# Matmul with batch norm: the last half chunk of the last column tile as one piece of 256 rows instead of two of 128

## The chip, the cores and the metric

The kernel runs on one core of a Trainium2 chip. The metric is the device time of one execution in microseconds; five runs of the kernel before have a median of 211.6 us (211.12 to 212.11).

## The reference

```python
batch, m, k, n = 16, 512, 1024, 768
y = np.matmul(x, weight)                       # x: (16, 512, 1024), weight: (1024, 768), float32
mean = np.mean(y, axis=(0, 1), keepdims=True)
var = np.var(y, axis=(0, 1), keepdims=True)
y_norm = (y - mean) / np.sqrt(var + eps)
return (gamma * y_norm + beta).astype(np.float32)
```

Mean and variance of each of the 768 columns go over all 8192 rows, so no column can be normalised before its last row has been multiplied. The output is 25.2 MB.

## The kernel before, in words

The 8192 rows are cut into 16 chunks of 512 (`C`, `CH`); half a chunk has 256 rows (`QR`). The 768 columns are six tiles of 128 (`NT`). The first two tiles are computed with rows on the partitions; the other four are column tiles: `y` lies transposed, with the tile's 128 columns on the partitions and the rows along the free dimension, so that statistics are taken along a partition. Each column tile goes through all chunks. For each chunk TensorE adds up eight matmuls into a PSUM bank, VectorE takes statistics of the bank (`bn_stats`), ScalarE copies it as bf16 into a `y` buffer (`keep`). When a tile's 16 chunks are done, the statistics are merged (`bn_aggr`), ScalarE takes the root, VectorE forms scale and shift. Then blocks of the tile are normalised in place, turned back to rows (transpositions on TensorE or by DMA), copied as float32 by ScalarE and stored through SP's queue. All of that but the last tile's goes on while TensorE multiplies the next tile.

The last tile (`nt = NT - 1`) has nothing to hide behind, so its end is made small:

- Its chunks 0 to 14 are as above. The last chunk, 15, is cut into `PIECES`, each with its own PSUM bank, matmuls, statistics and copy (`last_unit`, L694 on; the matmuls have line 705, the statistics 712, the copy 715). Before, the pieces are 256, 128 and 128 rows.
- The statistics of chunks 0 to 13 are merged early into the first three columns of `fin` (`sum_up`, L1145 to L1147). Chunk 14's go into the next six (L662), each piece's into six more. One `bn_aggr` over all of `fin` (`aggregate`, L1150) gives the tile's mean and variance. The `root` (L1153, ScalarE) follows, and on VectorE `first_term` (L1156) and `affine` (L1160 to L1162: reciprocal, scale, shift).
- Then blocks of this tile (`ends`): two of 256 rows, two of 512, six of 1024 and one of 512, each normalised (L1185, VectorE), turned (L1008, TensorE), copied (L1198, ScalarE) and stored (L1201, SP).
- One block of the tile before, of 1024 rows (`HELD = 1`), is held back until here. Its norm is done long before; its eight transpositions (L1008) stand on TensorE behind the last piece, its copy is line 1082 (ScalarE), its store line 1074 (SP, 512 KB).

No order of work is written by hand. Each step is a task with a due time, the engines it may use with an assumed occupation, and what it depends on. `arrange` runs an assumed timetable: in each round it takes the engine that can begin first, and among the tasks that can begin on it within 0.2 us (`LOOK`) the one with the smallest due time. It assumes 0.06 us from the end of a task to the start of one that depends on it (`SEM`). The instructions are then issued in this order, and each engine keeps it. The tasks around the change are:

```python
t = pe_task(0.92 * rows / QR, emit, waits(range(JW), c, 0, QPC), takes=[slot], uses=[x_slot[c]])
b = task(clock[0] - 40, dve(0.05 + 0.3 * rows / QR), bn, [t], uses=[slot])
k = task(clock[0] + 0.5, act(0.05 + 0.22 * rows / QR), keep, [b, col_end[nt, c - 1][1]], uses=[slot, y_of(nt, c)])
...
ag = task(E - 50.0, dve(0.25), aggregate,
ro = task(E - 50.0, {"ACT": (0.2, 0.3)}, root, [ag])
...
    b = col_block(hn, hc, E + 0.3 + 0.3 * i, hf)
    b.deps.append(col_end[nt, C - 1, len(PIECES) - 1][0])
```

`clock[0]` is the sum of TensorE's assumed occupations so far, `E` its value at the end of the last piece. A VectorE task ends 0.09 us after its occupation, one of TensorE 0.03. The last line makes the planner count the held block's transpositions (0.0555 us each) from the last piece's statistics on; the instructions themselves do not wait for these.

Of the kernel before, what the change touches and what calls it, by code (L numbers as in the profile page):

```python
# [227 lines left out]
def kernel(  # L228
# [10 lines left out]
    f32 = mybir.dt.float32  # L239
# [8 lines left out]
    P = 128  # L248
# [5 lines left out]
    QR = 256  # L254
    QPC = CH // QR
    JW = KQ // 64
    WAKE = 30
    FILL = 8
    EARLY = 4
# [1 line left out]
    GA = 2  # L261
    NA = GA * P
    GY = 2
    PAD = 34
    HELD = 1
    ASTAT = {2:tuple(range(4,16))}
    RC = C - 2
# [11 lines left out]
    singles = ctx.enter_context(tc.tile_pool(name="singles", bufs=1))  # L279
# [25 lines left out]
    ring = singles.tile([P, RING], f32)  # L305
    w_sb = singles.tile([P, JW, 2, N], bf16)
    eps_sb = singles.tile([P, 1], f32)
# [11 lines left out]
        seq(nc.vector.memset(acc, 0.0))  # L319
    tot = singles.tile([P, 2, NA], f32)  # L320
    stats = singles.tile([P, (NT - GA) * C + PAD, 6], f32)
    fin = singles.tile([P, 27], f32)
    psums = {nt: singles.tile([P, 2, C], f32, name=f"psums{nt}") for nt in ASTAT}
    sums = {nt: singles.tile([P, 4 + 6 * C], f32, name=f"sums{nt}") for nt in ASTAT}
    for nt in ASTAT:
# [18 lines left out]
    def task(prio, engines, emit, deps=(), lock=False, **kw):  # L344
        t = Task(prio, engines, emit, deps, **kw)
        t.lock = lock
        tasks.append(t)
        return t

    def dve(occ):  # L350
        return {"DVE": (occ, occ + 0.09)}
# [7 lines left out]
    def pe(occ):  # L359
        return {"PE": (occ, occ + 0.03)}  # L360
# [10 lines left out]
    def load_w(jw, jw1):  # L371
        def emit(eng):
            rows = weight.rearrange("(i jw c e) n -> i c jw (e n)", i=4, jw=JW, e=2)
            dst = w_sb.rearrange("p jw e n -> p jw (e n)")
            for i in range(4):
                seq(nc.gpsimd.dma_start(dst[32 * i:32 * i + 32, jw:jw1], rows[i, :, jw:jw1]))
# [18 lines left out]
    def turn_x(xslot, slot, m0, t0, jw0, jw1, new, rows=QR):  # L395
        def emit(eng):
            if new:
                xT_sb = xtpool.tile([P, JW, CH, 2], bf16, tag="xT")
                slot.tile = xT_sb
            half, row = divmod((m0 + 32 * t0) % CH, QR)  # L400
            src = xslot.tile[:, t0:t0 + rows // 32].rearrange("p t k -> p (t k)").bitcast(f32)
            src = src.rearrange("p (t jw c) -> p t jw c", jw=JW, c=32)
            dst = slot.tile.rearrange("p jw m e -> p (jw m e)").bitcast(f32)
            dst = dst.rearrange("p (jw q t r) -> p q t jw r", jw=JW, q=QPC, r=32)
            dst = dst[:, half, row // 32:(row + rows) // 32, jw0:jw1]
# [10 lines left out]
    for kind, n, *n1 in order:  # L416
        if kind == "w":
# [3 lines left out]
            t += 2.1 * (n1[0] - n)  # L421
            if n1[0] == JW:
                task(t, {"POOL": (0.6, 0.6)}, lambda eng: make_identity(nc, ident))
# [117 lines left out]
    def wake(count, slot):  # L541
        def emit(eng):
            idle_ps = psum.tile([P, CH], f32, tag="b")
            for _ in range(count):
                seq(nc.tensor.matmul(idle_ps, idle_sb[:, 0:P], idle_sb, start=True, stop=True))  # L545
        return emit
# [31 lines left out]
    def col_unit(nt, c, jws, q0=0, q1=QPC):  # L578
        slot = bank_of.setdefault((nt, c), None) or Slot(banks)
        bank_of[nt, c] = slot  # L580
        first = jws[0] == 0 and q0 == 0
        xs = [plain[c][0][jw] for jw in jws] if c in plain else [x_slot[c]]
        kw = {"takes": [slot], "uses": xs} if first else {"uses": [slot] + xs}
        t = pe_task((1.728 if c in plain else 1.808) * len(jws) / JW * (q1 - q0) / QPC,
                    mm(nt, c, list(jws), slot, q0, q1),
                    waits(jws, c, q0, q1) + ([plain[c][1][jw] for jw in jws] if c in plain else []), (nt, c), **kw)
        if q1 - q0 == QPC:
            t.hosts = 4
        if jws[-1] == JW - 1 and q1 == QPC:
            col_stats(nt, c, slot, t)  # L590
        return t
# [98 lines left out]
            k.deps.append(col_end[nt, c - 1][1])  # L690
        col_end[nt, c] = b, k

    PIECES = (0, QR), (QR, P), (QR + P, P)

    def last_unit(q):
        nt, c = NT - 1, C - 1
        r0, rows = PIECES[q]
        slot = Slot(banks)

        def emit(eng):  # L700
            y_ps = psum.tile([P, CH], f32, tag="b")
            slot.tile = y_ps
            for jw in range(JW):
                for e in range(2):
                    seq(nc.tensor.matmul(  # L705
                        y_ps[:, 0:rows], w_sb[:, jw, e, nt * P:(nt + 1) * P],
                        x_slot[c].tile[:, jw, r0:r0 + rows, e],
                        start=(jw == 0 and e == 0), stop=(jw == JW - 1 and e == 1),
                    ))

        def bn(eng):
            seq(nc.vector.bn_stats(fin[:, 9 + 6 * q:15 + 6 * q], slot.tile[:, 0:rows]))

        def keep(eng):
            seq(nc.scalar.copy(y(nt, c)[:, r0:r0 + rows], slot.tile[:, 0:rows]))
# [4 lines that stand above are left out]
        col_end[nt, c, q] = b, k  # L720


    wake_slot = Slot(banks)
    task(1.0, pe(0.217 * WAKE), wake(WAKE, wake_slot), takes=[wake_slot])

# [410 lines left out]
    for c in range(EARLY, C - 1):  # L1136
        for jws in halves:
            col_unit(nt, c, jws)
    for q in range(len(PIECES)):
        last_unit(q)  # L1140
# [18 lines left out]
    def affine(eng):  # L1159
# [6 lines left out]
    ag = task(E - 50.0, dve(0.25), aggregate,  # L1166
              [su, col_end[nt, C - 2][0]] + [col_end[nt, C - 1, q][0] for q in range(len(PIECES))])
    ro = task(E - 50.0, {"ACT": (0.2, 0.3)}, root, [ag])
    ft = task(E - 50.0, dve(0.1), first_term, [ag])
    af = task(E - 50.0, dve(0.45), affine, [ro, ft])  # L1170
    for i, (hn, hc, hf) in enumerate(held):
        b = col_block(hn, hc, E + 0.3 + 0.3 * i, hf)
        b.deps.append(col_end[nt, C - 1, len(PIECES) - 1][0])
    ends = [(0, 0, QR), (0, QR, QR), (1, 0, CH), (2, 0, CH)] + [(c, 0, 2 * CH) for c in range(3, C - 1, 2)]
    ends += [(C - 1, 0, CH)]
    for c, r0, rows in ends:
        due = E + 2.0 + 0.6 * c
        n = max(rows // CH, 1)
        keeps = [col_end[nt, c + i][1] for i in range(n) if c + i < C - 1]
        keeps += [col_end[nt, C - 1, q][1] for q in range(len(PIECES))] if c + n == C else []  # L1180
        norms = []
# [67 lines left out]
```

## Time and profile before

| | |
|---|---|
| median of five runs | 211.6 us (211.12 to 212.11) |
| the profiled execution: its own time | 212.11 us |
| its span, first to last instruction | 209.8 us |
| mean granted TensorE clock | 0.981 |
| busy: TensorE, VectorE, ScalarE, GpSimd | 192.9, 140.2, 153.8, 107.5 us |
| matmuls of the last chunk (L705): first start | 188.20 us |
| root of the last tile (L1153): start | 190.88 us |
| last copy of ScalarE: end | 200.2 us |
| transfers: last packets | 208.2 us |

A row of the profile names the line of the kernel, the engine, the operation, what is written from what, the shape, and how many instructions were merged (x24). PE is TensorE's matmul, PEld its weight load, DVE is VectorE, ACT ScalarE, POOL GpSimd; SPq is SP's queue, which issues the stores. In a timeline row the first number is the start and the second the length, in microseconds from the span's start; what ended an idle stretch stands in brackets. In a row of a group the numbers behind the bar are the busy time in us and the mean length of one instruction in ns. A window's row gives the busy time of each engine in it, then the clock, the share of the 16 DMA engines and GB/s. A matmul's record is longer than its share of TensorE, since matmuls overlap; how fast they follow each other is read from their starts.

The transfers of the program's own code are queues of the kind "instruction" in the profile: q8 has ten packets, 0.16 MB, and q14 seven, 0.06 MB.

### The profile page before, as it was taken

The numbers are of one execution on the slowest core, as the hardware profiler recorded it, in microseconds if no ns is written. First come the engines' busy times: TensorE is split into PE (matmuls) and PEld (weight loads), VectorE is DVE, ScalarE is ACT, GpSimd is POOL, SyncE is SP. The second block draws the span as 40 slices with busy tenths as digits, with TensorE's granted clock in tenths as the row PEclk, the third lists the DMA queues.
The fourth block names the chain that finished last, engine by engine and source line by source line (L and its number), as shares of the span: only waits on it lengthen the run. The fifth ranks groups of instructions, "written<-read, shape, count | busy, mean of one in ns | idle before, by whom it ended". The sixth has DMA issues, their size and how long they took to land.

```text
span 209.8 us, 3519 instructions
## 1 busy us (share of the span) xinstructions
PE 192.9 (92%) x1242; PEld 114.8 (55%) x1242; DVE 140.2 (67%) x230; ACT 153.8 (73%) x264; POOL 107.5 (51%) x130
## 2 busy tenths in 40 slices
PE   7988999999999999999999999999999999997600
PEld 2355554856568888776864444444444455545400
DVE  4220887787879899768879999854963594348500
ACT  2000665999999999989778987999676768878910
POOL 7777957697858999999106986750000000000000
PEclk9999999999999999999999999999999999999975
DMA  5999999999999999999004799999999999999994
GB/s 56 165 164 196 195 196 196 196 197 196 191 195 195 196 197 196 196 197 189 14 0 158 262 386 351 297 343 317 266 274 236 325 325 336 254 348 308 344 345 144
DMA packets 95137, 47.95 MB, mean 229 GB/s; under 512 B 20880, under 2 KB 94608, under 8 KB 95120
## 3 DMA queue, kind: packets, MB, share of 16 engines
q0 software_dynamic: 34688, 18.36, 64.1%
q1 hardware_dynamic: 60432, 29.37, 50.8%
q8 instruction: 10, 0.16, 0.3%
q14 instruction: 7, 0.06, 0.1%
HBM read 36.71 MB, written 25.17 MB: 295 GB/s over the span
## 4 chain that ended last, share of the span: by engine, by line
PE 78%; DMA 10%; ACT 3%; DVE 1%; issue 1%; POOL 1%; ACTq 0%; DVEq 0%; POOLq 0%
PE y_ps L529 50%; PE y_ps L467 21%; DMA ring<-in_x_dram 8%; PE y_ps L767 4%; ACT o_sb L1198 3%; DMA w_sb<-in_weight_dram 3%; PE o_ps L1008 2%; POOL ring L385 1%; PE y_ps L705 1%; DVE xT_sb L406 1%; PE a_ps L872 0%; ACTq L1244 0%; PE o_ps L1038 0%; PE tot_ps L825 0%; DVE y_sb L1185 0%
## 5 line engine op out<-in xcount | busy, mean ns | idle before, releaser
L529 PEld LDWEIGHTS <-w_sb 128*128 128x128 bf16 x512 | 49.4, 97 | 59.1
L529 PE MATMUL y_ps<-xT_sb,w_sb 128*128 128x512 bf16 (+1 forms) x256 | 59.5, 380 | 0.0
L529 PE MATMUL y_ps<-x_pl,w_sb 128*128 128x512 bf16 x256 | 58.7, 379 | 0.0
L385 POOL DMA_DIRECT2D ring<-in_x_dram x76 | 47.4, 628 | 12.7 <-DMA ring<-in_x_dram 4.6
L467 PE MATMUL y_ps<-w_sb,xT_sb 128*128 128x256 bf16 x448 | 50.7, 273 | 2.0 <-DVE xT_sb L406 1.3
L406 DVE STREAM_TRANSPOSE xT_sb<-ring 128x1024 f32<-128x1024 f32 (+1 forms) x35 | 38.3, 1131 | 17.2 <-DMA ring<-in_x_dram 17.2
L467 PEld LDWEIGHTS <-xT_sb 128*128 128x128 bf16 x448 | 43.5, 98 | 9.9 <-DVE xT_sb L406 2.0
L662 DVE BATCH_NORM_STATS2 stats<-y_ps 128x6 f32<-128x512 f32 x46 | 31.5, 691 | 23.0 <-PE y_ps L529 22.8
L666 ACT CAST y_sb<-y_ps 128x512 bf16<-128x512 f32 x51 | 29.0, 592 | 11.7 <-DVE stats L662 10.0
L501 ACT COPY x_pl<-xT_sb 128x1024 bf16<-128x1024 bf16 x32 | 32.4, 1050 | 2.3 <-DVE xT_sb L406 2.3
L610 ACT ACTIVATE sq_sb<-y_ps 128x512 f32<-128x512 f32 x28 | 16.6, 603 | 22.0 <-PE y_ps L467 21.4
L906 POOL TENSOR_TENSOR ring<-ring,sum 128x1024 f32<-128x1024 f32 (+1 forms) x11 | 23.7, 2179 | 17.4 <-DVE ring L901 16.8
L617 POOL TENSOR_TENSOR sum<-sum,sq_sb 128x512 f32<-128x512 f32 x22 | 28.2, 1280 | 2.4 <-ACT sq_sb L610 1.5
L613 DVE TENSOR_TENSOR sum<-y_ps,sum 128x512 f32<-128x512 f32 x28 | 18.9, 675 | 10.3 <-ACT sq_sb L610 9.2
L1008 PE MATMUL o_ps<-ident,y_sb 128*128 128x128 bf16 x128 | 17.6, 220 | 1.5 <-DVE y_sb L1185 1.5
L623 ACT CAST y_sb<-y_ps 128x512 bf16<-128x512 f32 x28 | 15.8, 589 | 3.2 <-DVE sum L613 3.1
L901 DVE TENSOR_TENSOR ring<-y_sb,a_ps 128x1024 f32<-128x1024 bf16 (+1 forms) x16 | 16.9, 1080 | 1.1 <-DMA out_dram<-ring 0.8
L1104 ACT CAST ring<-ring 128x1024 f32<-128x1024 bf16 x16 | 16.8, 1052 | 0.2 <-DMA ring<-y_sb 0.2
L545 PE MATMUL idle_ps<-idle_sb 128*128 128x512 bf16 x38 | 11.5, 472 | 1.2 <-DVE idle_sb L310 1.2
L1008 PEld LDWEIGHTS <-y_sb 128*128 128x128 bf16 x128 | 9.4, 97 | 3.6 <-DVE y_sb L1185 1.9
L987 ACT ACTIVATE y_sb<-y_sb,shift,scale 128x1024 bf16<-128x1024 bf16 x8 | 9.8, 1245 | 0.0
L1082 ACT CAST ring<-o_ps 128x1024 f32<-128x1024 bf16 x8 | 8.0, 1017 | 1.3 <-PE o_ps L1008 0.8
(89 smaller groups left out, 121.3 us busy)
## 6 DMA issues: line engine op xcount, KB each, us to landing
out_dram<-ring SPq DMA_DIRECT2D x38, 512.0 KB, 3.9
ring<-in_x_dram POOLq DMA_DIRECT2D x52, 256.0 KB, 9.4
out_dram<-o_sb SPq DMA_DIRECT2D x6, 512.0 KB, 6.0
ring<-in_x_dram POOLq DMA_DIRECT2D x16, 128.0 KB, 5.5
out_dram<-ring SPq DMA_DIRECT2D x4, 256.0 KB, 2.2
w_sb<-in_weight_dram POOLq DMA_DIRECT2D x8, 96.0 KB, 5.1
w_sb<-in_weight_dram POOLq DMA_DIRECT2D x4, 192.0 KB, 5.4
ring<-in_x_dram POOLq DMA_DIRECT2D x4, 192.0 KB, 7.6
```

The lines of the kernel that those rows point to most:

```text
L385: seq(nc.gpsimd.dma_start(x_bf[32 * i:32 * i + 32], src[:, :, KQ * i:KQ * (i + 1)]))
L406: seq(nc.vector.transpose(dst, src[:, :, jw0:jw1]))
L467: seq(nc.tensor.matmul(y_ps[:, s], x_slot[c].tile[:, jw, t * P:(t + 1) * P, e], w_sb[:, jw, e, 0:NA], start=(s == 0 and jw == 0 and e == 0 ...
L501: seq(nc.scalar.copy(dst, pairs) if eng == "ACT" else ENG[eng].tensor_copy(dst, pairs))
L529: seq(nc.tensor.matmul(y_ps, w_sb[:, jw, e, nt * P:(nt + 1) * P], moving(c, jw, e, q0 * QR, q1 * QR, parted), start=(jw == 0 and e == 0 an ...
L613: seq(nc.vector.tensor_add(sum1, slot.tile[:, 0:n], sum1))
L617: seq(ENG[eng].tensor_add(acc, acc, state["sq"][:, 0:n]))
L662: seq(nc.vector.bn_stats(dst, slot.tile))
L666: seq(nc.scalar.copy(y(nt, c), slot.tile))
L901: seq(nc.vector.tensor_mul(slot.o, y_row[c].y[:, s0:s1], aff[0][:, None, :].to_broadcast([P, n, NA])))
L906: seq(ENG[eng].tensor_add(slot.o, slot.o, row[:, None, :].to_broadcast([P, n, NA])))
L1008: seq(nc.tensor.transpose(dst, src, ident))
```

## The change

The last chunk's second half is one piece of 256 rows instead of two of 128. `PIECES` moves to the constants at the head of the kernel; `fin` has room for two pieces instead of three (21 columns instead of 27), and `stats` two entries of padding more.

```diff
+    PIECES = ((0,QR),(QR,QR))
...
-    PAD = 34
+    PAD = 36
...
     stats = singles.tile([P, (NT - GA) * C + PAD, 6], f32)
-    fin = singles.tile([P, 27], f32)
+    fin = singles.tile([P, 9 + 6 * len(PIECES)], f32)
...
-    PIECES = (0, QR), (QR, P), (QR + P, P)
```

In instructions: of the last chunk's 24 matmuls with 24 weight loads, 16 of each are left, of its three statistics and three copies two of each. Each piece works in a PSUM bank of its own, so that one bank fewer is taken.

## The prediction

> **What bounds the kernel now.** I read the page's chain of waits first. It gives 78% to TensorE, but it follows the last instruction back through issue times, so for the end of the run it has to be held against the transfers. I therefore read, for the last 20 us: the timeline, the busy times by quarter microsecond, the groups by shape, and the DMA queues in short windows. Times are from the span's start; those with three decimals are single records of the trace.
>
> The windows (length, then PE, PEld, DVE, ACT and POOL busy, clock, DMA share, GB/s):
>
> ```profile
> 192.25:192.50 0.25, 0.25 (x4) 0.11 (x2) 0.25 (x2) 0.05 (x1) 0.00 (x0) 1.00 1.03 295
> 192.50:192.75 0.25, 0.21 (x3) 0.05 (x2) 0.25 (x2) 0.25 (x2) 0.00 (x0) 1.00 0.05 14
> 192.75:193.00 0.25, 0.25 (x4) 0.18 (x4) 0.25 (x2) 0.25 (x2) 0.00 (x0) 1.00 0.00 0
> 193.00:193.25 0.25, 0.25 (x6) 0.22 (x4) 0.25 (x2) 0.20 (x2) 0.00 (x0) 1.00 0.86 262
> 206.00:206.50 0.50, 0.00 (x0) 0.00 (x0) 0.00 (x0) 0.00 (x0) 0.00 (x0) 0.50 1.15 349
> 207.00:207.50 0.50, 0.00 (x0) 0.00 (x0) 0.00 (x0) 0.00 (x0) 0.00 (x0) 0.50 0.07 22
> ```
>
> The reader is to see three things. The stores run dry at about 192.5 and start again at 193.0. From there to about 206.6 they move 345 GB/s without a break (ScalarE, which feeds them, is done at 200.2). The last 1.5 us, to 208.2, belong to a remnant at 22 GB/s, one sixteenth of the full rate. Nothing behind 193.0 waits for an engine, so the end moves one for one with the moment at which stores start again. That moment is set here:
>
> ```profile
> 188.20 1.99 PE L705 MATMUL y_ps<-xT_sb,w_sb 128*128 128x256 bf16 x24
> 190.03 0.61 PE L1008 MATMUL o_ps<-ident,y_sb 128*128 128x128 bf16 x8
> 190.23 0.30 DVE L712 BATCH_NORM_STATS2 fin<-y_ps 128x6 f32<-128x128 f32 x1 [0.16 <-PE y_ps L705]
> 190.56 0.27 ACT L715 CAST y_sb<-y_ps 128x128 bf16<-128x128 f32 x1 [0.20 <-DVE fin L712]
> 190.56 0.28 DVE L1150 BATCH_NORM_AGGREGATE mv<-fin 128x2 f32<-128x27 f32 x1
> 190.88 0.29 ACT L1153 ACTIVATE std<-mv,eps_sb 128x1 f32<-128x1 f32 x1
> 191.08 0.99 ACT L1082 CAST ring<-o_ps 128x1024 f32<-128x1024 bf16 x1
> ...
> 192.09 0.37 SPq L1074 DMA_DIRECT2D out_dram<-ring  x1
> 192.85 0.37 SPq L1201 DMA_DIRECT2D out_dram<-o_sb  x1
> ```
>
> The first store after the dry stretch is not one of the last tile: it is the held block's (L1074, 512 KB), issued at 192.09. Its copy (L1082) stands on ScalarE behind the root (L1153), and the root waits for the aggregate (L1150). The first store of the last tile (L1201, 192.85) comes 0.76 us later, and the held 512 KB keep the wires busy for 1.5 us at 345 GB/s, so that branch (reciprocal, scale, shift, norm, turn, copy) has some 0.7 us of slack. What decides is last matmul, L712, L1150, L1153, L1082, L1074.
>
> **The change part by part.** The groups by shape:
>
> ```profile
> L705 PE MATMUL y_ps<-xT_sb,w_sb 128*128 128x128 bf16 x16 | 1.1, 219 | 0.0
> L705 PE MATMUL y_ps<-xT_sb,w_sb 128*128 128x256 bf16 x8 | 1.1, 275 | 0.0
> L712 DVE BATCH_NORM_STATS2 fin<-y_ps 128x6 f32<-128x128 f32 x2 | 0.6, 298 | 0.2 <-PE y_ps L705 0.2
> L712 DVE BATCH_NORM_STATS2 fin<-y_ps 128x6 f32<-128x256 f32 x1 | 0.4, 431 | 0.2 <-PE y_ps L705 0.2
> L715 ACT CAST y_sb<-y_ps 128x128 bf16<-128x128 f32 x2 | 0.5, 265 | 0.2 <-DVE fin L712 0.2
> L715 ACT CAST y_sb<-y_ps 128x256 bf16<-128x256 f32 x1 | 0.4, 372 | 0.1
> ```
>
> TensorE: 16 matmuls of 128 columns become 8 of 256. Start to start, the eight wide ones now there take 113.3 ns each (188.202 to 189.108), the 16 narrow ones 57.8 ns (189.108 to 190.033). So 8 x 113.3 = 907 ns replace 925. The last result is ready at the last start plus its recorded duration: 189.108 + 7 x 0.1133 + 0.275 = 190.176 instead of 190.193, that is -0.02 us. Here a rule of the Trainium skill speaks for a large gain: "TensorE: Matmul & The Clock Gate", section Back-to-back issue gap, has pairs of weight load and matmul sustain about 81 ns at 128 columns and 131 at 512. Estimated by it (98 ns at 256 between the two), the sum would be 8 x 98 - 16 x 81 = -0.51 us. The row has 57.8 where the rule has 81, at full granted clock, so I take -0.02.
>
> Statistics on the path: the last L712 covers 256 columns instead of 128: 431 - 298 = +0.13 us. The L712 of the middle piece (0.30 us from 189.77) falls away, but it lies beside the last matmuls, which run until 190.19; it gains nothing. If those were shorter than it, it would have been worth up to 0.30.
>
> Aggregate: 21 inputs instead of 27. The row of 84 inputs (L1146) takes 533 ns, that of 27 takes 279: 4.5 ns an input, so -0.03 us. The trace's other aggregates over 27 take 240 and 260, so between 0 and -0.06.
>
> ScalarE: the middle piece's copy (265 ns from 190.10) goes; ScalarE was idle for 0.20 us behind it, so nothing is gained. The last copy is 372 instead of 265 ns and stands in front of the root. With L712 at 190.21 to 190.64, the copy runs 190.68 to 191.05, and the aggregate ends at 190.93; root ready at 190.965. Is it held up until 191.05? Copies of this size follow each other after 268 ns (192.452, 192.720), L1082 started 0.09 us before the root's record ended, and the middle copy, which waited for VectorE, started 0.04 us before the one ahead of it ended. 190.678 + 0.268 = 190.946 is earlier than 190.965, so I take 0; without any overlap it would be 191.10, or +0.13 more. Queued behind the root are L1082 and all copies of the last tile; they shift by as much.
>
> Order: the planner sums 0.92 us of TensorE either way, so E and the due times hang where they were. In its own figures the root is ready 0.46 us after the last statistic (aggregate 0.34, two signals of 0.06), the held copy 0.59 (eight turns 0.474, two signals), and the root is the more urgent; the order copy, root, held copy stays. No DMA is added or moved, and SP's and POOL's queues keep their order. The wider `stats` and narrower `fin` only move bytes; statistics of one shape into different tiles take 679 to 700 ns, so 0.
>
> Sum: -0.017 + 0.133 - 0.027 = +0.09 us on the root, hence on the held store; the dry stretch gets longer by it. Against its own run: span 209.84 to 209.93, run 212.11 to 212.20. That run was the slowest of five, 0.5 above their median; on the median, 211.6 becomes 211.7. Bounds of the unknown terms: +0.05 (aggregate) to +0.22 (no overlap).
>
> **The rivals.**
>
> 1. The shift is hidden: 211.6. If stores were still queued at 193.0, +0.09 would vanish. The window with 0 GB/s speaks against it.
>
> 2. Slower: an instruction block moves into the drain. The queues in 192 to 193 us and in 198.3 to 199.5 show
>
> ```profile
> q14 instruction: 1, 0.01, 3.4%
> ...
> q8 instruction: 1, 0.02, 4.9%
> ```
>
> The first is some 8 KB, from 192.448 for 0.55 us, just inside the dry stretch; the second 16 KB, from 198.468 for 0.95 us, inside the drain. I read the 1.5 us remnant as the work of the one DMA engine that carried the 16 KB packet. If 8 KB cost half as much and, ScalarE's stream being one instruction shorter, were fetched after 193.0 instead of 192.45 on that same engine, the end comes 0.75 + 0.09 = 0.84 us later: 212.4. That is where it decides: 193.0. For it: 0.5 us of distance. Against: ScalarE's three fetches begin after 57, 182 and 315 of its records; if they are called at a fixed distance of 128, the call is at record 182 - 128 = 54 at the latest, for the third at 310 at the latest (189.77), in front of the removed copy.
>
> 3. Faster: the 16 KB block of TensorE's stream is no longer fetched. "Runtime: NRT & Kernel Launch", section Instruction fetch mechanics, says that code comes in 16 KiB blocks of 256 instructions by a DMA queue of the sequencer's own and that crossing a block is "mostly hidden"; by it this is worth 0, by the row of the remnant up to 1.5 us, and the time 211.7 - 1.4 = 210.3. Sixteen instructions fewer could drop the last block. Against it: the ten packets begin at 213, 467, 701, 980, 1230, 1446, 1703, 1963, 2231 and 2517 of TensorE's records; with steps of 256, the sixth puts the call at 166 at the latest, so the tenth at 2470 at the latest, and 2501 remain. It comes about 0.5 us later, still inside the drain.
>
> **How the numbers follow.** A change of 0.3% (0.63 us) is about what a measurement of this kernel can tell from no change. The sum: 0.52, of which nearly all stays within 0.3%; hidden: 0.05; slower by a moved block, or by an unforeseen loss of its kind in the drain: 0.30; faster by a lost block: 0.13. That gives faster 0.13, same 0.56, slower 0.31. The likeliest is 211.7, by itself 211.2 to 212.1 with the scatter of the five runs. The range takes in rival 2 with its scatter and leaves rival 3 out: 211.1 to 212.6.
>
> **What would show it.** Right: eight wide L705 in the last piece 113 ns apart, last L712 about 431 ns, L1150 near 252, root near 190.97, L1074 near 192.18, stores again near 193.1, the same slope to the end. The step on ScalarE is wrong if the root starts only when the copy's record has ended. Rival 2 shows an 8 KB packet behind 193.0 and a remnant of 2 us or more; rival 3 only nine 16 KB packets and hardly a remnant. The forecast as a whole fails if the remnant changes its length for another reason: it is worth seventeen times the sum.

## The result, and the profile after

The changed kernel takes 211.14 us in the median of 43 runs (209.91 to 213.02), the kernel before 212.02 us of 80 in the same comparison: ratio 0.9961, 95% interval 0.995 to 0.9972. It is faster by 0.4%, where no change was forecast; of the three rivals it is the third that came. The runs of both scatter by 0.5 to 0.7 us, so ratios below stand with their intervals.

The groups by shape of the last chunk after the change (TensorE's matmuls, then statistics, copies, aggregate; busy us, mean ns of one, idle before):

```profile
L705 PE MATMUL y_ps<-xT_sb,w_sb 128*128 128x256 bf16 x16 | 2.0, 275 | 0.0
L712 DVE BATCH_NORM_STATS2 fin<-y_ps 128x6 f32<-128x256 f32 x2 | 0.9, 432 | 0.7 <-PE y_ps L705 0.7
L715 ACT CAST y_sb<-y_ps 128x256 bf16<-128x256 f32 x2 | 0.7, 372 | 0.6 <-DVE fin L712 0.5
L1150 DVE BATCH_NORM_AGGREGATE mv<-fin 128x2 f32<-128x21 f32 x1 | 0.2, 249 | 0.0
```

The timeline of the same stretch:

```profile
187.01 1.98 PE L705 MATMUL y_ps<-xT_sb,w_sb 128*128 128x256 bf16 x16
...
189.03 0.43 DVE L712 BATCH_NORM_STATS2 fin<-y_ps 128x6 f32<-128x256 f32 x1 [0.48 <-PE y_ps L705]
189.49 0.37 ACT L715 CAST y_sb<-y_ps 128x256 bf16<-128x256 f32 x1 [0.54 <-DVE fin L712]
189.49 0.25 DVE L1150 BATCH_NORM_AGGREGATE mv<-fin 128x2 f32<-128x21 f32 x1
...
189.78 0.29 ACT L1153 ACTIVATE std<-mv,eps_sb 128x1 f32<-128x1 f32 x1
189.98 0.99 ACT L1082 CAST ring<-o_ps 128x1024 f32<-128x1024 bf16 x1
```

The path does what the sum said. From the first L705 to the root it takes 2.76 us (187.01 to 189.78), where it took 2.68 before (188.20 to 190.88): +0.09. The root starts at 189.776, 0.035 us behind the end of the aggregate as before, while the copy's record runs until 189.864; so it is not held up.

That the whole stretch lies 1.2 us earlier is not the change: the two programs are the same up to line 705, and the kernels below, equal up to there as well, have the first L705 between 187.2 and 188.3 (the changed kernel itself at 188.34 in e9). The start of the run varies by that much. So all places in the drain are counted from the first L705 from here on.

The end, in windows (busy times, clock, DMA share, GB/s):

```profile
191.50:191.75 0.25, 0.21 (x5) 0.15 (x4) 0.25 (x2) 0.25 (x2) 0.00 (x0) 1.00 0.02 4
191.75:192.00 0.25, 0.25 (x6) 0.15 (x5) 0.25 (x2) 0.25 (x1) 0.00 (x0) 1.00 0.22 70
...
205.00:205.50 0.50, 0.00 (x0) 0.00 (x0) 0.00 (x0) 0.00 (x0) 0.00 (x0) 0.50 1.14 347
205.50:206.00 0.50, 0.00 (x0) 0.00 (x0) 0.00 (x0) 0.00 (x0) 0.00 (x0) 0.50 0.19 51
206.00:206.50 0.50, 0.00 (x0) 0.00 (x0) 0.00 (x0) 0.00 (x0) 0.00 (x0) 0.50 0.00 0
```

The dry stretch is there (4.30 to 4.92 us behind the first L705, before 4.26 to 4.84), the full rate lasts until 18.6 us (before 18.5), and then nothing is left: the remnant of 1.5 us at 22 GB/s is gone. The page's third part says what went with it; first the kernel before, then the changed one:

```profile
q8 instruction: 10, 0.16, 0.3%
```

```profile
q8 instruction: 9, 0.15, 0.3%
```

Nine blocks of code instead of ten. The tenth is not saved but comes behind the stores: it begins at 208.40, 1.0 us behind the end of the span.

### The profile page after: what moved, and what is told of

It reads as the page before. It is cut to its first block, busy times and chain, and to the rows that moved or that the text cites. A ratio compares the mean times of both kernels' runs of the same rounds, so it can differ in the third digit from the quotient of the medians.

```text
span 207.4 us, 3501 instructions
## 1 busy us (share of the span) xinstructions
PE 192.2 (93%) x1234; PEld 114.5 (55%) x1234; DVE 140.0 (68%) x229; ACT 153.7 (74%) x263; POOL 107.5 (52%) x130
## 4 chain that ended last, share of the span: by engine, by line
PE 79%; DMA 6%; POOL 5%; ACT 3%; DVE 1%; issue 1%; ACTq 0%; POOLq 0%; DVEq 0%
PE y_ps L530 50%; PE y_ps L468 21%; PE y_ps L767 4%; ACT o_sb L1198 3%; DMA ring<-in_x_dram 3%; DMA w_sb<-in_weight_dram 3%; POOL w_sb L377 3%; POOL ring L386 2%; PE o_ps L1008 2%; PE y_ps L705 1%; DVE xT_sb L407 1%; PE a_ps L872 0%; ACTq L1244 0%; PE o_ps L1038 0%; PE tot_ps L825 0%
## 5 line engine op out<-in xcount | busy, mean ns | idle before, releaser
L663 DVE BATCH_NORM_STATS2 stats<-y_ps 128x6 f32<-128x512 f32 x46 | 31.5, 691 | 22.9 <-PE y_ps L530 22.5
L667 ACT CAST y_sb<-y_ps 128x512 bf16<-128x512 f32 x51 | 29.1, 592 | 11.6 <-DVE stats L663 10.0
L614 DVE TENSOR_TENSOR sum<-y_ps,sum 128x512 f32<-128x512 f32 x28 | 18.9, 675 | 10.3 <-ACT sq_sb L611 9.2
L546 PE MATMUL idle_ps<-idle_sb 128*128 128x512 bf16 x38 | 10.8, 451 | 1.2 <-DVE idle_sb L311 1.2
```

The source lines that it names most:

```text
L614: seq(nc.vector.tensor_add(sum1, slot.tile[:, 0:n], sum1))
L663: seq(nc.vector.bn_stats(dst, slot.tile))
L667: seq(nc.scalar.copy(y(nt, c), slot.tile))
```

## The experiments

Theory A: TensorE's code comes in blocks of 16 KB; with 16 instructions fewer the tenth is no longer fetched while the stores drain, and the one DMA engine that carried it no longer ends 1.5 us behind the others. Theory B: fewer and larger instructions on the way to the last statistics make the gain. The table gives for each profile: instructions of TensorE's stream against the kernel before; when the tenth block began; when the root did; when the stores had dropped below half of their rate for good (all three in us behind the first L705); the remnant behind that; and the ratio of the timed runs to the kernel before. The times are worked out of single records. "None" means none within the span; in the changed kernel, e7, e16 and e17 the records show the tenth block behind the span's end, at 20.9 to 22.9 us.

| kernel | stream | block | root | full rate to | remnant | ratio (95%) |
|---|---|---|---|---|---|---|
| before | 0 | 10.3 | 2.68 | 18.5 | 1.5 | 1 |
| e8, the same again | 0 | 10.4 | 2.68 | 18.5 | 1.5 | 0.9992 (0.9968 to 1.0016) |
| after | -16 | none | 2.76 | 18.6 | 0.1 | 0.9961 (0.995 to 0.9972) |
| e9, the same again | -16 | 10.7 | 2.76 | 18.7 | 1.6 | 0.9949 (0.9923 to 0.9975) |
| e6, two pieces, tail 2 | -12 | 11.4 | 2.77 | 18.6 | 1.4 | 0.9984 (0.9967 to 1.0001) |
| e4, two pieces, tail 4 | -8 | 11.4 | 2.76 | 18.6 | 1.4 | 0.9981 (0.9964 to 0.9999) |
| e1, two pieces, tail 8 | 0 | 11.6 | 2.76 | 18.7 | 1.7 | 0.9983 (0.9969 to 0.9998) |
| e5, three pieces, tail 8 | +16 | 10.2 | 2.67 | 18.5 | 1.5 | 0.9974 (0.9961 to 0.9987) |
| e2, three, no fill | -16 | none | 2.67 | 18.5 | 0.2 | 0.9933 (0.9906 to 0.996) |
| e3, three, no fill, tail 8 | 0 | 11.3 | 2.67 | 18.5 | 1.4 | 0.9976 (0.996 to 0.9992) |
| e10, three, wake 22 | -16 | none | 2.67 | 18.5 | 0.2 | 0.9964 (0.9935 to 0.9993) |
| e14, three, wake 22, fill 4 | -24 | none | 2.67 | 18.9 | 0.4 | 0.9962 (0.9938 to 0.9986) |
| e13, two, wake 22 | -32 | none | 2.76 | 18.6 | 0.1 | 0.9955 (0.9929 to 0.9982) |
| e12, one piece | -32 | none | 3.22 | 19.0 | 0.1 | 0.9952 (0.9934 to 0.997) |
| e15, 384 and 128 rows | -16 | none | 2.69 | 18.5 | 0.1 | 0.9932 (0.9907 to 0.9958) |
| e7, three, no fill, halves | -16 | none | 3.00 | 18.4 | 0.3 | 0.9982 (0.9964 to 1.0) |
| e11, three, wake 22, halves | -16 | 10.4 | 3.00 | 18.5 | 1.6 | 0.9987 (0.9962 to 1.0013) |
| e16, two, halves | -16 | none | 2.94 | 18.3 | 0.1 | 0.9935 (0.9911 to 0.9959) |
| e17, 384 and 128, halves | -16 | none | 3.17 | 18.8 | 0.1 | 0.9951 (0.9925 to 0.9978) |

**The stream made longer or shorter away from the path (e1 to e6).** "Tail" adds idle matmuls behind the last transposition (two instructions each), where TensorE has nothing left to do; "no fill" leaves out the eight idle matmuls near 12 us and nothing else.

```diff
 # e1 (after), e5 (before): 8; e4: 4; e6: 2
     for t in order:
         t.emit(t.engine)
+    wake(8, None)(None)
 # e2, e3 (before; e3 also with the tail of 8)
-    pe_task(0.217 * FILL, wake(FILL, fill_slot), [w_ready[0]], takes=[fill_slot])
+    pe_task(0.217 * FILL, lambda eng: None, [w_ready[0]], takes=[fill_slot])
```

> Two pieces, and eight idle matmuls (with their weight loads 16 instructions) appended behind TensorE's last transposition, so that its stream is as long again as before the change; TensorE is idle there. Theory A (the change drops a 16 KB block of code from the drain): the tenth q8 packet is back at about 198 us, a remnant of some 1.5 us follows the other transfers, and the time is that of the kernel before, 0.996 of it at most by 0.3% noise: ratio to before 1.000, 0.4% slower than after. Theory B (the gain comes from fewer and larger instructions on the way to the last statistics): nothing on that way has changed, ratio to before 0.996.

> Three pieces as before, but the eight idle matmuls that fill TensorE's wait for x near 12 us are not issued (the timetable still counts them), so that its stream is 16 instructions shorter, as after the change. Theory A: nine q8 packets within the span, no remnant, ratio to before 0.995 to 0.996. Theory B: the pieces are as before, ratio 1.000. A start that gets slower without the idle matmuls would show in the start of the first matmul of line 705.

> As the kernel without the eight idle matmuls near 12 us, but with eight behind TensorE's last transposition: three pieces, stream as long as before. Both theories expect 1.000; with theory A the tenth packet and the remnant are there. It is the control for leaving out the idle matmuls at the start: if it is below 0.998, that alone is worth something.

> Two pieces and four idle matmuls (8 instructions) behind the last transposition: half the distance between the two kernels. Theory A says only that the packet is either there or not, with either 1.000 or 0.996, and nothing between; it tells in which half of the 16 instructions the call for the block stands. Theory B: 0.996.

> The kernel before, with eight idle matmuls behind TensorE's last transposition. If these are free and the block of code is in the drain with them or without: ratio 1.000, remnant about 1.5 us. The two kernels with such a tail came out at 0.998 with a remnant of 1.4 to 1.7 us in their profiles; if the idle matmuls themselves gain something (the call for the block comes later), this one is 0.998 too. Theory B: 1.000.

> Two pieces and two idle matmuls (4 instructions) behind the last transposition. Theory A: the packet is there (0.998 to 1.000, remnant about 1.5 us) or not (0.996, hardly a remnant), according to which side of the boundary 4 instructions reach; the four-matmul kernel has it. Theory B: 0.996.

Block and remnant go together in every profile: ten of ten blocks and 1.4 to 1.7 us wherever the stream is longer than that of the changed kernel, two pieces or three, and neither in e2 with its three pieces:

```profile
span 208.8 us, 3488 instructions
...
q8 instruction: 9, 0.15, 0.3%
```

With four instructions more than the changed kernel (e6, one profile) the block is there:

```profile
span 210.0 us, 3505 instructions
...
q8 instruction: 10, 0.16, 0.3%
```

What the block does to the stores shows in the kernel before, in windows ahead of it, during it (198.47 to 199.42) and behind it:

```profile
196.97:198.46 1.49, 0.66 (x9) 0.39 (x8) 0.20 (x1) 1.49 (x2) 0.00 (x0) 1.00 1.14 345
198.47:199.42 0.95, 0.00 (x0) 0.00 (x0) 0.00 (x0) 0.95 (x2) 0.00 (x0) 1.00 1.08 326
200.00:201.40 1.40, 0.00 (x0) 0.00 (x0) 0.00 (x0) 0.21 (x1) 0.00 (x0) 1.00 1.15 347
```

The stores fall from 345 to 326 GB/s while it runs, about one sixteenth (15/16 of 345 is 323), as if one of the 16 engines carried no stores. The other eight profiles with the block show the same: 340 to 347 GB/s ahead of it, 324 to 329 during it.

The times were less clean. The kernels with a tail came out at 0.998 instead of 1.000, also e5, whose profile is that of the kernel before. Most of it lies outside the span: a run takes 2.4 us longer than its span for the kernel before, 2.0 us for the five with a tail (medians), so about their whole 0.2% (0.4 us) has nothing to do with the drain. What makes it was not tried. The spans alone say it more clearly: the mean span of each of the five lies within 0.1 us of that of the kernel before in the same comparison, with two pieces (e1, e4, e6) as with three (e3, e5), while e2's is 1.3 us shorter.

**The same kernels again, and a cleaner cut (e8 to e10).**

```diff
 # e10 (before)
-    task(1.0, pe(0.217 * WAKE), wake(WAKE, wake_slot), takes=[wake_slot])
+    task(1.0, pe(0.217 * WAKE), wake(WAKE - 8, wake_slot), takes=[wake_slot])
```

> The kernel before, unchanged, timed as the others are. Four kernels whose code block is in the drain as in the kernel before came out between 0.9974 and 0.9984. If that is a gain of their own (the idle matmuls), this one has 1.000; if the comparison itself leans by that much, this one has about 0.998, and all ratios so far are to be read against it.

> The changed kernel, unchanged. Theory A, with the profiles' remnant of 1.4 us less the longer path of 0.1 us: 0.6% below the unchanged kernel of the same call. The first measurement of the change says 0.4%. Theory B: 0.4% or less, with nothing in the drain to explain it.

> Three pieces, and 22 instead of 30 idle matmuls at the very start: TensorE's stream is 16 instructions shorter, as with the change, but its wait near 12 us is filled as before, so that the clock does not fall as it did in two of the three kernels without that filling. Theory A: no tenth packet, hardly a remnant, root 2.67 us behind the first matmul of the last chunk, time at or 0.1 us under that of the changed kernel. Theory B: as the unchanged kernel of this call.

The kernel before against itself gives 0.9992. The surprise is e9: the very kernel of the change, and this time its profile has the tenth block (ten packets on q8), 10.7 us behind the first L705, and behind the full rate the remnant:

```profile
206.50:207.00 0.50, 0.00 (x0) 0.00 (x0) 0.00 (x0) 0.00 (x0) 0.00 (x0) 0.50 1.12 337
207.00:207.50 0.50, 0.00 (x0) 0.00 (x0) 0.00 (x0) 0.00 (x0) 0.00 (x0) 0.50 0.15 42
207.50:208.00 0.50, 0.00 (x0) 0.00 (x0) 0.00 (x0) 0.00 (x0) 0.00 (x0) 0.50 0.07 22
208.00:208.50 0.50, 0.00 (x0) 0.00 (x0) 0.00 (x0) 0.00 (x0) 0.00 (x0) 0.50 0.07 23
208.50:209.00 0.50, 0.00 (x0) 0.00 (x0) 0.00 (x0) 0.00 (x0) 0.00 (x0) 0.50 0.01 3
```

So the changed kernel stands on the boundary: the block comes in some executions. Of the nine profiles of kernels with 16 instructions fewer, two have it (e9, e11). That fits the size of the gain. The remnant lost less the longer path would be 1.3 us in the profiles; the spans of the timed runs differ by 1.1 (mean 208.58 of 44 runs, 209.67 of the 196 runs of the kernel before beside the experiments). That is as if about one run in six still had it, an estimate so rough that none or one in three would fit as well. The spans scatter by 0.72 us, against 0.41 to 0.62 in the kernel before and the kernels with a tail. How often the block comes was not counted.

**Clear of the boundary (e12 to e14).**

```diff
 # e12 (after)
-    PIECES = ((0,QR),(QR,QR))
-    PAD = 36
+    PIECES = ((0,CH),)
+    PAD = 37
 # e13 (after), e14 (before): wake(WAKE - 8, wake_slot); e14 also wake(FILL - 4, fill_slot)
```

> The whole last chunk as one piece of 512 rows (eight matmuls, one statistic, one copy): another 16 instructions fewer in TensorE's tail, and the nearest step further in the direction of the change. Theory A, now with a boundary that the changed kernel stands on (its tenth block was fetched in the drain in one of its two profiles): no tenth block in the drain in any run, span of the runs 1.4 us shorter for it than with it. Its path is longer: statistics 700 instead of 431 ns, copy 585 instead of 372 ns in front of the root, so the root 3.1 to 3.3 us behind the first matmul of the chunk and stores again 0.3 to 0.5 us later. Sum against the unchanged kernel: about -1.4 + 0.1 + 0.4 = -0.9 us, ratio 0.995 to 0.997. Theory B (fewer and larger instructions on the path are what gains): faster than the changed kernel.

> Two pieces and 22 instead of 30 idle matmuls at the start: 32 instructions fewer than before, 16 fewer than with the change. Theory A with the boundary: the tenth block is never fetched in the drain, so the spans of the timed runs scatter less (standard deviation about 0.5 us, where the changed kernel has 0.7) and their mean is 0.2 to 0.4 us below that of the changed kernel (208.6): ratio 0.993 to 0.995. If the changed kernel's wider scatter has another source, mean and scatter stay as they are.

> Three pieces, with 22 instead of 30 idle matmuls at the start and four instead of eight near 12 us: 24 instructions fewer than before, 8 fewer than with the change. Theory A with the boundary: as the kernel with two pieces and 22 idle matmuls, 0.1 us faster by its shorter path: 0.993 to 0.995, standard deviation of the spans about 0.5 us. Three pieces with 16 fewer had the tenth block in one of four profiles. Theory B: 1.000.

Theory B asks that one piece be faster than the changed kernel by way of a shorter path. The path does not get shorter:

```profile
187.49 1.97 PE L705 MATMUL y_ps<-xT_sb,w_sb 128*128 128x512 bf16 x8
189.50 0.70 DVE L712 BATCH_NORM_STATS2 fin<-y_ps 128x6 f32<-128x512 f32 x1 [1.11 <-PE y_ps L705]
190.23 0.58 ACT L715 CAST y_sb<-y_ps 128x512 bf16<-128x512 f32 x1 [1.22 <-DVE fin L712]
190.23 0.22 DVE L1150 BATCH_NORM_AGGREGATE mv<-fin 128x2 f32<-128x15 f32 x1
190.71 0.30 ACT L1153 ACTIVATE std<-mv,eps_sb 128x1 f32<-128x1 f32 x1
```

Its root is 0.54 us later than before the change (here the copy does hold it up: ready at 190.49, it starts at 190.71), and its full rate lasts 0.55 us longer, one for one. Yet it gains 0.5%, since the remnant is gone (its ratio and that of the changed kernel are not told apart); and its spans scatter by only 0.37 us. e13 and e14 have no block in the drain either, but neither mean (208.7 and 208.6) nor scatter (0.68 and 0.80) fell as expected. They cut at the start, and that moves the ninth block too: from 8.3 us in front of the first L705 to 6.3 to 6.7, into the transposing transfers there. In e10 the stores then stand still longer than before the change (first e10, then the kernel before):

```profile
181.00:182.00 1.00, 1.00 (x10) 0.54 (x8) 0.00 (x0) 1.00 (x3) 0.00 (x0) 1.00 2.45 210
182.00:183.00 1.00, 1.00 (x9) 0.52 (x8) 0.60 (x1) 0.48 (x1) 0.00 (x0) 1.00 0.07 7
```

```profile
181.00:182.00 1.00, 1.00 (x10) 0.51 (x8) 0.15 (x1) 1.00 (x2) 0.00 (x0) 1.00 2.29 202
182.00:183.00 1.00, 1.00 (x9) 0.55 (x8) 0.30 (x1) 0.78 (x2) 0.00 (x0) 1.00 0.20 40
```

So they are no clean test of the boundary, and the wide scatter of the changed kernel is explained by it only as far as e12 goes.

**The last piece's length, and the dry stretch (e7, e11, e15 to e17).** e15 keeps the changed kernel's stream and gives the last piece 128 rows. "Halves" copies and stores the held block as two of 512 rows, the first copy in front of the root.

```diff
 # e15, e17 (after)
-    PIECES = ((0,QR),(QR,QR))
+    PIECES = ((0,QR+P),(QR+P,P))
 # e7 (as e2), e11 (as e10), e16 (after), e17 (as e15): the held block
-        b = col_block(hn, hc, E + 0.3 + 0.3 * i, hf)
-        b.deps.append(col_end[nt, C - 1, len(PIECES) - 1][0])
...
+        b, bank = turn_block(due + 0.5, hn, m0, count, [a], [yslot])
+        b.deps.append(col_end[nt, C - 1, 0][0])
...
+        for h, prio in ((0, E - 60.0), (1, due + 1.0)):
+            copy, store = half(h)
+            d = task(prio, act(0.47), copy, [b], takes=[slot] if h == 0 else [], uses=[bank] if h == 0 else [bank, slot])
```

> Three pieces, the eight idle matmuls near 12 us not issued (no block in the drain), and the held block copied and stored in two halves, the first in front of the root on ScalarE, the second behind it. It tests the claim that the end moves with the moment at which stores start again. If so, the stretch without stores (0.14 to 0.6 us in the profiles so far) closes, the transfers run at 345 GB/s from before the root to the end, and the kernel gains 0.15 to 0.5 us on the same one with the whole copy: 0.991 to 0.993. The root itself comes some 0.2 to 0.3 us later; were the last tile's own path the bound, it would lose that: 0.994 to 0.995.

> The same, and the held block copied and stored in two halves, the first in front of the root. Tests again that the end moves with the moment at which stores start again: the stretch without stores closes; if it is 0.5 us long without the split, the kernel gains up to 0.5 us (0.25%) on the one with the whole copy. If the last tile's own path counted, the root's delay of 0.3 us would show instead.

> Two pieces of 384 and 128 rows: TensorE's stream is as short as with the change (16 matmuls in the last chunk), and the last statistics cover 128 columns as before the change. If stream length and the last piece's length act apart: root 2.67 to 2.72 us behind the first matmul of the chunk (2.76 with the change), time 0 to 0.1 us under that of the changed kernel, ratio about 0.995; the block in the drain in few executions or none. If the gain were that of larger last instructions, it would be lost in part.

> The changed kernel with the held block copied and stored in two halves, the first in front of the root. Unlike the two earlier kernels with halves it leaves the start alone, so that the transfers around 181 us stay as they are and there is a stretch of 0.6 us without stores to close. If the end moves one for one with the moment at which stores start again: the stretch closes, the full rate ends 0.4 to 0.6 us earlier (about 18.1 us behind the first matmul of the chunk instead of 18.6), ratio 0.992 to 0.994. If the last tile's own path is the bound instead, the root's delay of 0.3 to 0.5 us shows: 0.996 to 0.998.

> Both together: 384 and 128 rows, held block in halves. By the sum of the two, 0.991 to 0.994, the fastest of all; by the rival of the last tile's own path 0.995 to 0.998.

e15 has the lowest ratio, with e2 and e16 level: 0.9932, 210.5 us in the median of six runs where the kernel before has 212.47. Its rows:

```profile
189.03 0.77 DVE L712 BATCH_NORM_STATS2 fin<-y_ps 128x6 f32<-128x384 f32 x2 [0.66 <-PE y_ps L705]
189.83 0.25 DVE L1150 BATCH_NORM_AGGREGATE mv<-fin 128x2 f32<-128x21 f32 x1
190.17 0.31 ACT L1153 ACTIVATE std<-mv,eps_sb 128x1 f32<-128x1 f32 x1
```

The root comes 2.69 us behind the first L705 (187.47) and the full rate ends at 18.5 us, so 0.07 of the changed kernel's 0.09 us is won back; that its ratio lies 0.003 under the changed one's is within the intervals.

The halves say how far "one for one" holds. In e16 the stretch without stores closes:

```profile
192.00:192.25 0.25, 0.25 (x4) 0.11 (x3) 0.25 (x2) 0.03 (x1) 0.00 (x0) 1.00 1.17 352
192.25:192.50 0.25, 0.21 (x3) 0.04 (x3) 0.25 (x2) 0.25 (x2) 0.00 (x0) 1.00 1.15 350
192.50:192.75 0.25, 0.25 (x4) 0.20 (x4) 0.25 (x2) 0.25 (x2) 0.00 (x0) 1.00 0.80 236
...
194.50:194.75 0.25, 0.25 (x5) 0.25 (x4) 0.25 (x2) 0.25 (x1) 0.00 (x0) 0.50 0.52 158
```

but the full rate ends only 0.27 us earlier than in the changed kernel, not 0.4 to 0.6: stores fall short again between 5.8 and 7.0 us (the last row is at 6.8). In e17 the root is 0.48 us later than in e15 and the full rate lasts 0.3 longer. Two causes stand side by side there. The root, and with it the last tile's blocks, are later; and TensorE's granted clock is 0.50 for 3.4 us, from 6.0 us on in e16 and from 4.4 in e17, while it turns these blocks. The clock falls in this way in eleven of the nineteen profiles, in six of the nine with the block and in five of the ten without, so it does not decide on the block. In e8, the kernel before, it falls from 5.8 us on; the last transposition ends at 10.06 instead of 9.43 us, and the full rate still ends at 18.5. With the halves it may cost something; the two causes were not told apart. So by their profiles the two gains do not add up; e17's ratio lies where the rival of the last tile's own path put it (0.995 to 0.998), with an interval that takes in the plain sum too (0.991 to 0.994). e16's ratio is as forecast, which a block that stayed away in its six runs would do nearly as well.

In e7 and e11 the longer stillness near 181 us had closed most of the stretch beforehand (0.1 us of it is left in e2 and e10), so nothing was left to win: their full rate ends at 18.4 and 18.5 us, as in e2 and e10. But their runs, for which a gain was forecast, lost: their mean spans are 0.7 us above those of e2 and e10 (209.22 and 208.47, 209.52 and 208.79). e11's profile has the block, e7's has not; whether it comes more often there was not counted, and the loss stays open.

## Why the prediction was wrong

- Path: right. TensorE 113 ns a matmul as predicted; last statistics 433 ns (431 said), aggregate 249 (252), no hold-up on ScalarE, root +0.09 us as summed. The 81 ns at 128 columns that the Trainium skill gives ("TensorE: Matmul & The Clock Gate", section Back-to-back issue gap) had promised 0.51 us here; 0.02 was measured.
- One for one: right for a later start (after +0.1, e12 +0.55), right only in part for an earlier one (e16). Whether the last tile's own path, for which 0.7 us of slack was said, is the bound there, or the half clock, stays open.
- Rival 1 and rival 2: not seen. The 8 KB packet of ScalarE still begins in the dry stretch (4.3 us behind the first L705 in both).
- The step that failed is in rival 3: "with steps of 256, the sixth puts the call at 166 at the latest, so the tenth at 2470 at the latest, and 2501 remain. It comes about 0.5 us later, still inside the drain." Rival 3 had 0.13 of the chances, and its price, up to 1.4 us, was right in the profile; but the bound took the block to be called when execution reaches a fixed place. With 2501 of these records the block stayed out of the drain in the changed kernel's first profile and came in e9; with 4 more it came (e6). So the call stands at 2501 or close to it, at least 31 behind the bound. By steps of 256 the sixth call would then stand at 2501 - 4 x 256 = 1477 or later, and its packet began when 1446 had been executed. So, if the steps are even, it was called ahead of execution, which a count of executed records misses. The Trainium skill gives TensorE a queue of 64 entries ("TensorE: Matmul & The Clock Gate", table at its head), which would leave room for 31; no run here isolates it. Why the tenth block is then not called as far ahead is not shown either. A bound taken in the middle of the run did not hold at its tail.
- Size: the profiles lose 1.4 us of remnant and add 0.1 of path, the timed runs lose 0.9 us. One part may be that the block still comes in some executions (e9). Another is outside the span: 2.54 us for the changed kernel, 2.4 before.

Theory A stands. Theory B fell with e2 (three pieces, yet a gain), with e1 beside e5 (two pieces, yet no gain where the block is there) and with e12 (a longer path, yet a gain).

## What to carry to other kernels

When the end of a kernel is a drain of stores at full rate, look at what else uses the DMA engines there: a single 16 KB block of code left 1.4 to 1.7 us of transfers behind the others, some sixteen times what the edit did to the path. A few instructions more or fewer in TensorE's stream can decide whether the block is fetched there, so an edit of such a kernel is judged only with the instruction queues of both profiles side by side, and with more than one profile if the boundary is near. Then the cut is worth making on purpose. At the start of the stream it moves the earlier blocks as well; the ratios do not tell the two places apart (0.993 to 0.996 in the tail and at the start).

## What was not expected of the hardware

- One profile does not tell for a kernel: the same program had nine blocks in its span once and ten once.
- Idle matmuls behind the last useful one shortened the time outside the span by 0.4 us (2.0 against 2.4), with nothing in the traces to say why.
- A 16 KB packet lasting 0.95 us leaves a remnant of 1.4 to 1.7 us. In the kernel before, seven packets of the 512 B kind right behind it took 65 to 85 ns each instead of 27, which is 0.3 us more; the rest stays open. That the remnant is the work of the engine that carried the block is inferred: the two come and go together, the stores lose one sixteenth while the block runs, and the remnant moves at one sixteenth of the full rate. The records do not name the engine.
